# Reordering the first stages of an encoder layer: later surveys, earlier gates, evenly spread side work

## The chip, the cores and the metric

The kernel runs on one core of a Trainium2 chip. The metric is the time of one execution on the device, in microseconds (us). The engines are TensorE (PE in the rows; PEld is its weight load), VectorE (DVE), ScalarE (ACT), GpSimd (POOL) and SyncE (SP), which issues most DMA transfers.

## The reference

One layer of an encoder over 1024 tokens of width 1024, with 256 memory tokens. Only the parts that the first stages of the kernel compute matter here:

```python
h = layer_norm(x, ln_in_w, ln_in_b)
z = h @ w_in + b_in          # q, k, v, o of 4 recurrent heads, 16 gate columns, q, k, v of 8 windowed heads
...
# recurrent heads: both directions, chunks of 128 tokens, log gates summed along the tokens
a = jnp.cumsum(lfc, axis=-1)
m_t = jnp.maximum(inter_log, jnp.max(d_log, axis=-1))
...
ml_out = jax.nn.sigmoid(mo) * (hn * ml_norm_w)
...
# cross-attention of every token into the memory
q = (x @ w_q)...; kv = mem @ w_kv; k, v = jnp.split(kv, 2, axis=-1)
s = jnp.einsum('bthd,bmhd->bhtm', q, k) * (XA_DIM ** -0.5)
o = jnp.einsum('bhtm,bmhd->bthd', p, v).reshape(b, t, d) @ w_o + b_o
```

After it come a gated feed-forward part with a depthwise convolution and a last normalisation. They take most of the kernel's time, and the change does not touch them.

## The kernel before

Almost every float32 product is made from 16-bit or rounded halves: an operand is split into a high half (`whi`, `Be`, `Bo`, ..., by ScalarE, L204 or L571) and a low half (by VectorE, L205, or L572 on VectorE or GpSimd), and a product is three matmuls (L225 high by high, L226 and L227 with one low half) for each slice of 128 rows. A split needs a power-of-two scale for its operand. For a token weight the scale is a short chain: ScalarE and VectorE bound the weight (L309, L311), TensorE spreads the maximum over the partitions (`mx`, L183), and VectorE takes it back (L184) and makes the scale (L175 to L177, L319).

The span before 284 us has two stages.

The **input stage** (L551 to L717) does four things at once. For n from 0 to 15 it makes one slice of the memory's keys or values: weight load L566, split L570 to L572, 24 matmuls into `mem`, eviction L590, maximum L591. It normalises the eight token tiles `x` (norm_a: statistics L238 to L242, a power on GpSimd L243, then L252, L253 on ScalarE, times the weight L256 on VectorE, plus the bias L257 on GpSimd) and transposes and splits them (norm_b: eight transposes L607, split L204 and L205 into `Be` or `Bo`, and the load of tile tt+3, since `x` has three buffers). For n from 8 on it makes the first token product of a tile (tok_item, `tk`, 24 matmuls of 272 columns for gates and values and 24 of 256 columns). And it surveys the cross-attention's weights: a transfer of 1 MB into `cr` (L631) and a maximum over it on VectorE (L633). The first token weight lies in `cr` before that, so a survey comes after its split.

The **chunk stage** (L798 to L840) makes four further chunks c of 256 columns for eight tiles tt: 24 matmuls into `tk`, eviction L814 into `ev`, and for c of 2 and 3 a sigmoid on ScalarE (L819) and a product on GpSimd (L820). Between them it places four kinds of side work, each a generator that is called forward: `kv`, the memory's heads (a weight `wr` of 1 MB L752, its split, matmuls into `mem`, evictions into `stage`, all for one of eight heads); `ts`, the T-sums (ten GpSimd operations L730 to L739 into the single buffer `tsum`, then the halves on ScalarE L742 and VectorE L743; eight groups, two calls each); `gg`, the gates' chain (matmuls L376 to L378, difference `g_sb` L383, transpose L386, a running maximum L394 and L395, rows L406 to L421); and the bounds and splits of the next token weight. `tk` and `mem` share their PSUM banks.

The order in the code is not the order on the engines: a scheduler that runs when the program is built sets each engine's own order from readiness and from the order in which the code emits its work. Each engine then runs its line in order, and an instruction that waits holds all that is queued behind it on that engine; a DMA that waits holds the queue of SP.

Of the kernel before, what the change touches and what calls it, by code (L numbers as in the profile page):

```python
# [56 lines left out]
def encoder(ctx, tc, I, out):  # L57
# [224 lines left out]
    with ExitStack() as ca:  # L282

        yml = None
        with ExitStack() as cm:
# [254 lines left out]
            with ExitStack() as c2:  # L540
# [12 lines left out]
                with ExitStack() as c1:  # L553
# [45 lines left out]
                    def norm_b(tt):  # L599
                        if tt >= NT:  # L600
                            return
                        r = xs.pop(tt)
                        o = slice(tt // 2 * 128, tt // 2 * 128 + 128)
                        for q in range(2):
                            pt = tbank()
                            for k in range(4):
                                T.transpose(pt[:, k, :], r[:, (4 * q + k) * 128:(4 * q + k + 1) * 128], ident)  # L607
                            split16(Bp[tt % 2][:, 0, q, :, o], Bp[tt % 2][:, 1, q, :, o], pt, s0)
                        load_x(tt + 3)
# [62 lines left out]
                    for n in range(8):  # L672
                        if n < 6:
                            split_w(n + 2)
                        if n == 7:
                            split_w(8)
                        kv_item(n)
                        load_w(n + 4)
                        if n == 0:
                            load_x(2)  # L680
                        if n in (2, 3):
                            next(gens[n - 2])
                        if n % 2:
                            norm_a(n // 2)
                            if n > 1:
                                norm_b(n // 2 - 1)
                        if n == 5:
                            next(gens[0])
                        if n == 7:
                            run(gens[0])  # L690
                            next(gens[1])
                    xv = mm.tile([128, 8, 256], F32, name="xvr", tag="xv")
                    for n in range(8, 16):
                        split_w(n + 1)
                        kv_item(n)
                        load_w(n + 4)
                        norm_a(n - 4)
                        norm_b(n - 5)
                        if n == 8:
                            run(gens[1])  # L700
                            nxt = chunk_gen(I["w_tok"][0], 256, cw)
                            next(nxt)
                        if n == 10:
                            pk, sk = scale_of(sums[:, 0:8], 14)
                            as_pairs(xk, "xk", sk, "kp")
                        if n == 15:
                            run(nxt)
                            nxt = chunk_gen(I["w_tok"][1], 256, cw)
                            next(nxt)
                        tok_item(n - 8)  # L710
                        survey(n - 8)
                        if n == 14:
                            next(nxt)
                    pv_, sv_ = scale_of(sums[:, 40:48], 14)
# [83 lines left out]
                with ExitStack() as c1:  # L798
# [5 lines left out]
                    kv, ts, gg, cu0 = kv_gen(), tsum_gen(w1), gate_gen(), cu_prep(0)  # L804
                    next(kv)
                    for c in range(4):
                        w, ic = cw[2 + c]
                        for tt in range(NT):
# [22 lines left out]
                                    next(cu0)  # L831
                            if c == 2 and tt == 4:
                                next(cu0)
                            if c == 1:
                                next(gg, None)
                            with tc.issue_after(d.ins):
                                next(ts, None)
                            if tt in (2, 6):
                                next(kv, None)
                    run(kv)  # L840

# [381 lines left out]
    with ExitStack() as cb_:  # L1223
# [515 lines left out]
        with ExitStack() as cF:  # L1739
# [49 lines left out]
            for tt in range(NT):  # L1789
# [13 lines left out]
                for i in range(2 if last else 1):  # L1803
                    c = slice(i * 512, i * 512 + 512) if last else slice(0, D)
# [88 lines left out]
```

## Time and profile before

| | |
|---|---|
| three runs | 1570.8, 1573.36, 1579.4 us; median 1573.36 |
| profiled execution | 1571.99 us, its span 1570.3 us, mean granted clock 0.976 |
| TensorE busy | 1476.7 us, 94% of the span |
| VectorE, ScalarE, GpSimd busy | 1053.8, 807.4, 574.6 us |
| input stage, chunk stage | 0 to 134.06, 134.06 to 283.74 us |

The rows name an instruction by its line, engine and operation, and by the tiles that it writes and reads (out<-in). A time in brackets is idle time of the engine just before the instruction, with what ended it.

### The profile page before, as it was taken

To read this page: it belongs to the slowest core of one execution; us is meant where nothing else is said; L and a number is where in the kernel's file an instruction comes from. 1 tells how busy PE (TensorE), PEld (TensorE's weight loads), DVE (VectorE), ACT (ScalarE), POOL (GpSimd) and SP (SyncE) were. 2 spreads that over 40 slices of the span, in tenths; PEclk is the share of its full clock that TensorE was granted. 3 is DMA by queue.
4 is the path that set the end of the run, shared out by engine and by line. 5 is a ranking of instruction groups with operands and counts; after the bars stand their busy time and mean duration, and the time that the engine had idled before them with its cause. 6 is when DMAs were issued, how large, how long until landed. Compare 5 with 4: busy or idle time off the path is not lost.

```text
span 1570.3 us, 21752 instructions
## 1 busy us (share of the span) xinstructions
PE 1476.7 (94%) x8134; PEld 881.3 (56%) x8134; DVE 1053.8 (67%) x1961; ACT 807.4 (51%) x1367; POOL 574.6 (37%) x446
## 2 busy tenths in 40 slices
PE   8798889999999899899999889999999999997998
PEld 6697767456766788774455434444444444443443
DVE  7984985445767777675457678788878878925333
ACT  5524544565554467523335668777777756611000
POOL 6423662412232766234112174444434420301342
PEclk9799999999999899999999989999999999998999
DMA  8743545323554743544001332222232434832111
GB/s 297 276 179 112 189 140 190 105 75 101 147 149 130 243 132 102 205 167 180 28 27 54 121 137 108 107 107 108 107 121 107 162 107 144 294 124 69 40 68 54
DMA packets 84896, 208.62 MB, mean 133 GB/s; under 512 B 7091, under 2 KB 36019, under 8 KB 81462
## 3 DMA queue, kind: packets, MB, share of 16 engines
q1 hardware_dynamic: 84496, 206.46, 37.9%
q8 instruction: 64, 1.05, 0.3%
q0 software_dynamic: 144, 0.49, 0.2%
q14 instruction: 42, 0.34, 0.1%
q10 hardware_dynamic: 150, 0.27, 0.0%
HBM read 158.34 MB, written 49.35 MB: 132 GB/s over the span
## 4 chain that ended last, share of the span: by engine, by line
PE 55%; DVE 20%; DMA 9%; ACT 9%; issue 4%; POOL 2%; SPq 1%; DVEq 0%; ACTq 0%; POOLq 0%
PE dn L227 5%; PE dn L226 5%; PE dn L225 5%; DMA sv<-in_w_down_dram 3%; PE S L225 3%; PE S L227 3%; PE S L226 3%; DVE wlo L205 3%; DVE cbuf L1586 2%; DVE cbuf L1587 2%; PE tk L225 2%; PE z L226 2%; PE z L227 2%; PE tk L226 2%; PE tk L227 2%
## 5 line engine op out<-in xcount | busy, mean ns | idle before, releaser
L225 PE MATMUL dn<-whi,yp 128*128 128x512 f16 x336 | 127.6, 383 | 1.4 <-ACT whi L204 1.4
L226 PE MATMUL dn<-wlo,yp 128*128 128x512 f16 x336 | 128.2, 382 | 0.0
L227 PE MATMUL dn<-whi,yp 128*128 128x512 f16 x336 | 128.2, 382 | 0.0
L1504 POOL TENSOR_TENSOR wraw<-ur 128x512 f32<-128x512 f32 x22 | 45.5, 2069 | 201.8 <-issue 187.3
L1586 DVE SCALAR_TENSOR_TENSOR cbuf<-C,wdw,cbuf 128x1024 f32<-128x1024 f32 x44 | 75.7, 1721 | 28.6 <-ACT cbuf L1585 28.5
L225 PEld LDWEIGHTS <-whi 128*128 128x128 f16 x540 | 53.6, 99 | 66.1 <-issue 7.7
L227 PEld LDWEIGHTS <-wlo 128*128 128x128 f16 x540 | 53.4, 99 | 59.8 <-DVE wlo L205 4.2
L226 PEld LDWEIGHTS <-whi 128*128 128x128 f16 x540 | 53.7, 99 | 54.6 <-issue 1.6
L205 DVE SCALAR_TENSOR_TENSOR wlo<-wraw,us,whi 128x1024 f16<-128x1024 f32 (+1 forms) x48 | 67.0, 1413 | 18.8 <-ACT whi L204 18.5
L253 ACT ACTIVATE r<-r,lnrs 128x1024 f32<-128x1024 f32 x19 | 23.6, 1243 | 101.7 <-DVE lnrs L252 101.7
L1587 DVE SCALAR_TENSOR_TENSOR cbuf<-C,wdw,cbuf 128x1024 f32<-128x1024 f32 x44 | 70.5, 1602 | 1.2
L204 ACT ACTIVATE whi<-wraw,us 128x1024 f16<-128x1024 f32 (+1 forms) x48 | 51.4, 1103 | 27.2 <-DVE us L177 22.3
L225 PEld LDWEIGHTS <-yp 128*128 128x128 f16 x352 | 34.6, 98 | 52.1 <-issue 11.5
L1585 ACT ACTIVATE cbuf<-C,bdw,wdw 128x1024 f32<-128x1024 f32 x44 | 54.5, 1238 | 10.5 <-DVE C L1622 9.7
L243 POOL TENSOR_TENSOR lnrs<-lnrs,mhalf 128x1 f32<-128x1 f32 x32 | 18.8, 589 | 110.7 <-DVE lnrs L242 93.1
L227 PEld LDWEIGHTS <-yp 128*128 128x128 f16 x352 | 34.6, 98 | 42.4 <-issue 1.4
L226 PEld LDWEIGHTS <-yp 128*128 128x128 f16 x352 | 34.7, 99 | 42.2 <-issue 1.4
L225 PE MATMUL tk<-whi,Bo 128*128 128x256 f16 (+1 forms) x192 | 53.6, 279 | 3.1 <-DVE stage L205 3.1
L226 PE MATMUL tk<-wlo,Be 128*128 128x256 f16 (+1 forms) x192 | 53.6, 279 | 2.1 <-DVE wlo L205 2.1
L225 PE MATMUL tk<-whi,Be 128*128 128x256 f16 (+1 forms) x192 | 53.9, 282 | 0.3 <-ACT whi L204 0.3
L227 PE MATMUL tk<-whi,Be 128*128 128x256 f16 (+1 forms) x192 | 53.6, 279 | 0.0
L226 PE MATMUL tk<-wlo,Bo 128*128 128x256 f16 (+1 forms) x192 | 53.2, 277 | 0.0
(496 smaller groups left out, 4855.4 us busy)
## 6 DMA issues: line engine op xcount, KB each, us to landing
ur<-in_w_up_dram SPq DMA_DIRECT2D x22, 1024.0 KB
sv<-in_w_down_dram SPq DMA_DIRECT2D x22, 512.0 KB
y<-cbuf SPq DMA_DIRECT2D x22, 512.0 KB
ur<-y SPq DMA_DIRECT2D x11, 1024.0 KB
wraw<-in_w_down_dram SPq DMA_DIRECT2D x22, 512.0 KB
r<-h SPq DMA_DIRECT2D x19, 512.0 KB
h<-r SPq DMA_DIRECT2D x16, 512.0 KB
wraw<-in_w_tok_dram SPq DMA_DIRECT2D x10, 512.0 KB
```

What stands on the lines that cost most here:

```text
L204: A.activation(hi, src, AF.Copy, scale=s)
L205: return V.scalar_tensor_tensor(lo, src, s, hi, op0=OP.mult, op1=OP.subtract)
L225: T.matmul(ps, lh, rh, start=first, stop=False, skip_group_check=skip)
L226: T.matmul(ps, lh, rl, start=False, stop=False, skip_group_check=skip)
L227: return T.matmul(ps, ll, rh, start=False, stop=last, skip_group_check=skip)
L243: G.tensor_tensor(rs[:, 0:1], rs[:, 0:1], mhalf[:, 0:1], OP.pow)
L253: A.activation(r, r, AF.Identity, scale=rs[:, 0:1], bias=rs[:, 1:2])
L1504: G.tensor_tensor(S1, A21, A22, OP.add)
L1585: A.activation(c, C[:, 1:SEQ + 1], AF.Identity, scale=wdw[:, 1, j:j + 1], bias=bdw[:, j:j + 1])
L1586: V.scalar_tensor_tensor(c, C[:, 0:SEQ], wdw[:, 0, j:j + 1], c, op0=OP.mult, op1=OP.add)
L1587: V.scalar_tensor_tensor(c, C[:, 2:SEQ + 2], wdw[:, 2, j:j + 1], c, op0=OP.mult, op1=OP.add)
```

## The change

No instruction is added or removed. In the input stage only tiles 0 to 2 are normalised, and only tile 0 is transposed, before n = 8; from then on a tile is normalised two steps before it is transposed. The surveys are placed at n from 10 to 15, the last four in pairs, instead of one at each n from 8 on. In the chunk stage the gates' chain is called at every second tile of the chunks 0 and 1 instead of at every tile of chunk 1; the T-sums at every odd tile of all four chunks instead of at every tile of the first two; the memory's heads at every second to fourth product instead of at two tiles of each chunk.

```diff
-                        if n % 2:
+                        if n in (1, 3, 5):
                             norm_a(n // 2)
-                            if n > 1:
-                                norm_b(n // 2 - 1)
                         if n == 5:
+                            norm_b(0)
                             next(gens[0])
...
-                        norm_a(n - 4)
-                        norm_b(n - 5)
+                        norm_a(n - 5)
+                        norm_b(n - 7)
...
-                        survey(n - 8)
+                        for i in {10: (0,), 11: (1,), 12: (2,), 13: (3,), 14: (4, 5), 15: (6, 7)}.get(n, ()):
+                            survey(i)
...
-                            if c == 1:
+                            if c < 2 and tt % 2 == 0:
                                 next(gg, None)
-                            with tc.issue_after(d.ins):
-                                next(ts, None)
-                            if tt in (2, 6):
+                            if tt % 2:
+                                with tc.issue_after(d.ins):
+                                    next(ts, None)
+                            if 8 * c + tt in (6, 10, 13, 16, 19, 22, 25, 28):
                                 next(kv, None)
```

On VectorE, where the scale of the first token weight is made (L184 to L319, with `us` the scale and `cr` the weight), this stood before:

```order
L184 TENSOR_REDUCE us<-mx 128x1
L242 TENSOR_SCALAR lnrs<-lnmv 128x1
L591 TENSOR_REDUCE sums<-xvr 128x1
L175 TENSOR_SCALAR us<-us 128x1
L238 BN_STATS lnst<-x 128x6 x2
L176 TENSOR_SCALAR us<-us 128x1
L240 BN_AGGR lnmv<-lnst 128x2
L177 TENSOR_SCALAR us<-us 128x1
L319 TENSOR_SCALAR us<-us,sc 128x1
L242 TENSOR_SCALAR lnrs<-lnmv 128x1
L252 TENSOR_SCALAR lnrs<-lnmv,lnrs 128x1 x2
L205 SCALAR_TENSOR_TENSOR wlo<-cr,us,whi 128x1088 x2
```

and this stands there now:

```order
L591 TENSOR_REDUCE sums<-xk 128x1
L572 TENSOR_TENSOR wlo<-wr_136,whi 128x1024
L591 TENSOR_REDUCE sums<-xk 128x1
L184 TENSOR_REDUCE us<-mx 128x1
L175 TENSOR_SCALAR us<-us 128x1
L176 TENSOR_SCALAR us<-us 128x1
L177 TENSOR_SCALAR us<-us 128x1
L319 TENSOR_SCALAR us<-us,sc 128x1
L591 TENSOR_REDUCE sums<-xk 128x1
L238 BN_STATS lnst<-x 128x6 x2
L311 TENSOR_TENSOR l_527<-l_527 128x1
L205 SCALAR_TENSOR_TENSOR wlo<-cr,us,whi 128x1088
```

The five steps of the scale now follow each other, between the maxima of the memory's keys instead of those of its values (`xk` comes before `xvr`). On TensorE the `mx` product of this scale stands behind 170 matmuls of the memory's slices, where before there were 218 and 24 transposes. The second token weight's scale still has other work between its steps: L184, L242, a survey's L633, L175.

On VectorE, at the gates' difference `g_sb` in the chunk stage, this stood before, in chunk 1:

```order
L205 SCALAR_TENSOR_TENSOR wlo<-wr,sc,whi 128x1024 x2
L814 SCALAR_TENSOR_TENSOR ev<-tk,us,btok_1473 128x256
L743 TENSOR_TENSOR TX1l<-tsum,TX1l 128x256 x2
L743 TENSOR_TENSOR TX1h<-tsum,TX1h 128x256
L814 SCALAR_TENSOR_TENSOR ev<-tk,us,btok_1473 128x256
L743 TENSOR_TENSOR TX1h<-tsum,TX1h 128x256
L380 COPY a_sb<-s 128x64
L381 COPY aend<-s 1x64
L383 TENSOR_TENSOR g_sb<-gates,a_sb 128x32 x2
```

and this stands there now, in chunk 0:

```order
L814 SCALAR_TENSOR_TENSOR ev<-tk,us,btok_1473 128x256
L380 COPY a_sb<-s 128x64
L381 COPY aend<-s 1x64
L383 TENSOR_TENSOR g_sb<-gates,a_sb 128x32 x2
L205 SCALAR_TENSOR_TENSOR wlo<-wr,sc,whi 128x1024
L814 SCALAR_TENSOR_TENSOR ev<-tk,us,btok_1473 128x256
L743 TENSOR_TENSOR TX1l<-tsum,TX1l 128x256
L743 TENSOR_TENSOR TX1h<-tsum,TX1h 128x256
L205 SCALAR_TENSOR_TENSOR wlo<-wr,sc,whi 128x1024
L814 SCALAR_TENSOR_TENSOR ev<-tk,us,btok_1473 128x256
L390 COPY cx_1689<-s 64x128
L311 TENSOR_TENSOR l_1555<-l_1555 128x1
```

The gates' difference now stands in front of the first memory head's split, and L311 of a coming token weight behind it. On TensorE the first memory product comes after seven token products of the stage instead of three.

On GpSimd the end of the chunk stage read before, behind the last group of T-sums:

```order
L736 TENSOR_TENSOR tsum<-Bo,tsum 128x256
L737 TENSOR_TENSOR tsum<-tsum,Bo 128x256
L738 TENSOR_TENSOR tsum<-Be,tsum 128x256
L739 TENSOR_TENSOR tsum<-tsum,Be 128x256
L820 TENSOR_TENSOR ev<-ev,mlw 128x256 x16
L471 TENSOR_TENSOR ev_3209<-wraw 128x512
```

and reads now:

```order
L734 TENSOR_TENSOR tsum<-tsum,Bo 128x256
L820 TENSOR_TENSOR ev<-ev,mlw 128x256
L732 TENSOR_TENSOR tsum<-tsum,Be 128x256
L735 TENSOR_TENSOR tsum<-tsum,Bo 128x256
L736 TENSOR_TENSOR tsum<-Bo,tsum 128x256
L737 TENSOR_TENSOR tsum<-tsum,Bo 128x256
L738 TENSOR_TENSOR tsum<-Be,tsum 128x256
L739 TENSOR_TENSOR tsum<-tsum,Be 128x256
L820 TENSOR_TENSOR ev<-ev,mlw 128x256 x3
L471 TENSOR_TENSOR ev_3209<-wraw 128x512
```

All sixteen L820 stood behind the last group; thirteen of them now stand within or between the last four groups.

## Rows read from the trace of the kernel before

**Rows 1.** TensorE's waits from 0 to 284 us, without those that a later group shows in the timeline alone or that the change doesn't meet: the waiting matmul, what it waited for, us in total, times, the longest.

```profile
PE mem L225 <- ACT whi L204: 5.5, 1, 5.5
PE tp L607 <- POOL x L257: 4.3, 2, 3.7
PE s L386 <- DVE g_sb L383: 4.2, 1, 4.2
...
PE tk L225 <- DVE stage L205: 3.1, 1, 3.1
...
PE mx L183 <- DVE l L311: 1.6, 1, 1.6
PE mem L225 <- ACT whi L571: 1.5, 1, 1.5
...
PE mem L225 <- DVE ev L814: 0.6, 1, 0.6
```

**Rows 2.** Busy time of each engine by stretch, with the granted clock of TensorE behind them, then the DMA share and GB/s. The columns: stretch, its length, then PE, PEld, DVE, ACT and POOL, each busy us and (instructions).

```profile
31.33:57.54 26.21, 20.42 (x149) 19.80 (x150) 21.74 (x41) 16.90 (x26) 14.11 (x8) 0.83 0.64 229
57.54:76.02 18.48, 14.33 (x90) 11.44 (x90) 18.39 (x28) 7.00 (x11) 7.05 (x4) 0.78 0.91 335
76.02:134.06 58.04, 58.04 (x496) 52.43 (x496) 40.58 (x63) 16.97 (x24) 16.99 (x16) 0.97 0.37 137
...
148.22:186.65 38.43, 34.25 (x300) 29.91 (x301) 30.63 (x49) 21.99 (x37) 23.87 (x27) 0.94 0.63 201
186.65:235.25 48.60, 43.10 (x341) 34.30 (x342) 40.84 (x91) 24.83 (x44) 31.88 (x38) 0.95 0.40 127
```

**Rows 3.** The timeline of TensorE at the first token product: start, duration, instruction, idle time before it.

```profile
53.05 1.97 PE L607 MATMUL tp<-ident,x 128*128 128x128 f32 x8 [3.72 <-POOL x L257]
...
57.54 0.38 PE L226 MATMUL tk<-wlo,Be 128*128 128x272 f16 x1 [2.07 <-DVE wlo L205]
```

**Rows 4.** The timeline of VectorE at the same place, with the first token weight's scale (`us`) and the split that it serves.

```profile
50.33 0.28 DVE L184 TENSOR_REDUCE us<-mx 128x1 f32<-128x128 f32 x1
...
50.98 1.27 DVE L238 BATCH_NORM_STATS2 lnst<-x 128x6 f32<-128x512 f32 x2
...
52.43 0.20 DVE L319 TENSOR_SCALAR us<-us,sc 128x1 f32<-128x1 f32 x1
...
54.18 4.57 DVE L205 SCALAR_TENSOR_TENSOR wlo<-cr,us,whi 128x1088 f16<-128x1088 f32 x2
```

**Rows 5.** Three stretches of 5 us, with the columns of rows 2.

```profile
55.00:60.00 5.00, 2.93 (x15) 1.74 (x13) 5.00 (x4) 3.25 (x4) 1.38 (x2) 0.50 0.40 119
...
185.00:190.00 5.00, 3.35 (x16) 2.42 (x17) 4.66 (x12) 1.89 (x2) 4.76 (x8) 0.51 0.72 274
205.00:210.00 5.00, 2.87 (x27) 2.58 (x28) 5.00 (x10) 2.12 (x4) 3.51 (x4) 1.00 0.79 285
```

**Rows 6.** The timeline of TensorE at its second long wait in the input stage.

```profile
72.33 1.88 PE L607 MATMUL tp<-ident,x 128*128 128x128 f32 x8 [3.13 <-DVE us L176]
```

**Rows 7.** The timeline of VectorE before it, with the second token weight's scale.

```profile
67.42 0.28 DVE L184 TENSOR_REDUCE us<-mx 128x1 f32<-128x128 f32 x1
...
68.21 2.27 DVE L633 TENSOR_REDUCE sums<-cr 128x1 f32<-128x2048 f32 x1
...
74.02 0.20 DVE L319 TENSOR_SCALAR us<-us,sc 128x1 f32<-128x1 f32 x1
```

**Rows 8.** VectorE's costliest line of the input stage, by line: count, busy us, mean ns of one, idle time before.

```profile
L633 DVE TENSOR_REDUCE sums<-cr 128x1 f32<-128x2048 f32 x8 | 18.1, 2267 | 0.0
```

**Rows 9.** The timeline of TensorE at its three long waits of the chunk stage.

```profile
148.22 0.39 PE L225 MATMUL mem<-xkp,whi 128*128 128x256 f16 x1 [5.46 <-ACT whi L204]
...
186.65 0.39 PE L386 MATMUL s<-ident,g_sb 128*64 128x128 f32 x1 [4.18 <-DVE g_sb L383]
...
207.13 0.28 PE L225 MATMUL tk<-whi,Bo 128*128 128x256 f16 x1 [3.14 <-DVE stage L205]
```

**Rows 10.** The timeline of VectorE at the split of the first memory head's weight.

```profile
148.19 2.98 DVE L205 SCALAR_TENSOR_TENSOR wlo<-wr,sc,whi 128x1024 f16<-128x1024 f32 x2 [3.64 <-ACT whi L204]
```

**Rows 11.** The timeline of TensorE at the end of the input stage: the first of the last token product's 24 matmuls, and the matmul that follows the last.

```profile
131.44 0.27 PE L225 MATMUL tk<-whi,Bo 128*128 128x256 f16 x1
...
134.06 0.61 PE L183 MATMUL mx<-ident,sc 128*128 128x128 f32 x4
```

**Rows 12.** The timeline of VectorE before the gates' transpose.

```profile
179.71 3.17 DVE L205 SCALAR_TENSOR_TENSOR wlo<-wr,sc,whi 128x1024 f16<-128x1024 f32 x2 [1.15 <-ACT whi L204]
...
185.28 1.23 DVE L383 TENSOR_TENSOR g_sb<-gates,a_sb 128x32 f32<-128x32 f32 x2
```

**Rows 13.** The timeline of VectorE before the third long wait of the chunk stage.

```profile
201.06 1.27 DVE L205 SCALAR_TENSOR_TENSOR wlo<-wraw,us,whi 128x1024 f16<-128x1024 f32 x1
202.26 2.46 DVE L205 SCALAR_TENSOR_TENSOR wlo<-wr,sc,whi 128x1024 f16<-128x1024 f32 x2
```

**Rows 14.** The timeline of GpSimd at the end of the chunk stage.

```profile
285.02 0.72 POOL L820 TENSOR_TENSOR ev<-ev,mlw 128x256 f32<-128x256 f32 x1 [7.08 <-ACT ev L819]
```

**Rows 15.** Single operations in the timeline of GpSimd: L736 of two T-sum groups, and an L820.

```profile
119.26 0.69 POOL L736 TENSOR_TENSOR tsum<-Bo,tsum 128x256 f32<-128x256 f16 x1
...
201.08 4.18 POOL L736 TENSOR_TENSOR tsum<-Bo,tsum 128x256 f32<-128x256 f16 x1
...
254.17 1.25 POOL L820 TENSOR_TENSOR ev<-ev,mlw 128x256 f32<-128x256 f32 x1 [4.62 <-ACT ev L819]
```

## The prediction, made before the changed kernel had run

> **What bounds the kernel now.** I began with the waits of TensorE over the first 284 us, because the change touches nothing later, then cut that time by stage, and then read VectorE, ScalarE and GpSimd around each long wait. By the waits [rows 1] TensorE stands still there some 33 us in all, and each long wait is ended by another engine's result, not by a transfer: by a split weight, a normalised tile, a scale, the gates. The stages [rows 2] show where: 149.7 us belong to the token products and the memory's heads (134.06 to 283.74), and the 45 us from 31.33 to 76.02 belong to the input stage, in which VectorE is busy 40.1 of 44.7 us while TensorE is busy 34.8. From 76.02 to 134.06 TensorE is busy throughout. What the change can win lies in two clusters: TensorE waiting for a saturated VectorE before 76 us, and TensorE waiting for things that come in bursts from 142 to 216 us.
>
> **Input stage.** Nothing is added or removed; instructions change places. At the first token product TensorE waits 3.72 us for a normalised tile and, after eight transposes, 2.07 us for the low half of the weight [rows 3]. Behind the second wait stands a chain on VectorE [rows 4]: its first step, the maximum over mx, begins at 50.33, the scale is finished at 52.63, and the split that follows is done at 58.75. Between those steps stand a normalisation's statistics (1.27 us), its aggregate and its L242, which belong to later tiles; the first product's own transposes wait for the tile's L256 and L257 behind them. In the order of the changed kernel the chain L184, L175, L176, L177, L319 is undivided and tiles 1 and 2 are normalised after it. Transposes of tiles 1 to 3 no longer precede the first product.
>
> So the first token product can start as soon as its weight is split. I carried the rows forward in the new order: the mx product falls after 170 instead of 218 products of the memory's inputs and 24 transposes; the first token product comes at about 48.1 us instead of 57.54, 9.4 us earlier, an estimate. Of these, 2.0 us are eight transposes at 1.97 us per eight [rows 3], which are only postponed. That leaves 7.4. The same from the other side: the two waits are 5.79 us, and while TensorE recovers its granted clock is 0.50 from 55 to 60 us [rows 5], where 2.93 us of busy work would take half at the upper level, 1.5 us more: 7.3.
>
> What is late next: the second cluster. It waits 3.13 us in front of the next transposes [rows 6], because the second chain on VectorE is spread from 67.42 to 74.22 [rows 7], with a survey of 2.27 us in the middle and two splits of transposed tiles and an L256 behind it. The new order still has a survey inside this chain (L184, L242, L633, L175), since the order is made from readiness and not from the place in the code. So I leave the second cluster where it is. The surveys cost VectorE 18.1 us, eight at 2267 ns [rows 8]; moving them helps only as far as they really leave the saturated time. New waits also come: a tile's transposes stand in front of token products with one product's lead, so each may wait for a normalised tile, as one does now for 0.6 us (4.3 less the longest, 3.7), or for a weight's high half, 1.5 us [rows 1]. I charge one of each, 2.1 us. Sum of the stage: -7.4 + 2.1 = -5.3. Bounds: if the second cluster's 3.13 us go too and nothing new comes, -10.5; if new waits take as much as the old ones and two weight waits more, +2.
>
> **Token products and memory's heads.** Three long waits lie here [rows 9]: 5.46 us before the first memory product, 4.18 us before the gates' transpose, 3.14 us before a token product; 0.6 us more is mem behind ev [rows 1]. The first: VectorE's half of the weight's split begins at 148.19, after 3.64 us of idle time for ScalarE's half [rows 10], while the memory product comes after three token products in TensorE's line. In the new order seven token products of 24 matmuls come first instead of three. The product before the stage's end takes 2.62 us (131.44 to 134.06, [rows 11]), so four more cover 10.5 us, more than the 5.46. The second wait: the gates' difference g_sb at 185.28 stands on VectorE behind a weight's split of 3.17 us, two evictions and the sums' low halves [rows 12]. In the new order it comes right behind its own inputs, in front of the first split of a memory head. The third, before 207.13, stands behind VectorE's splits of 1.27 us for a token weight and 2 x 1.2 for a memory head in one burst [rows 13], with the gates' rows between them; with heads at every third product the burst is divided. All four: 5.46 + 4.18 + 3.14 + 0.6 = 13.4 us.
>
> Clock: after the 4.18 us wait the granted clock is 0.51 from 185 to 190 us, yet 1.00 after the 3.14 us wait [rows 5]. Over the two stretches from 148.22 to 235.25 it is 0.94 and 0.95 [rows 2], which is 0.06 x 38.4 + 0.05 x 48.6 = 4.7 us if TensorE had work all that time. I count 3 of them as gone.
>
> New waits: VectorE now takes the first memory weight's split in front of evictions and of l_1555. When that split waits for its transfer, as it does now for 3.64 us, what is queued behind it is late: the evictions free the banks that token products write, and L311 feeds the mx product, which sits in TensorE's line. I price that at 1.8, the old mx wait being 1.6 [rows 1], plus 1.1 for the scan's result behind evictions and 0.7 for the second token weight of each chunk; between 2 and 3 us stay for the other four gaps of this size that I can't place, and 1 for the clock after them. Together 6.6 (from 2 to 13, since eight memory heads each bring one place to wait). Sum: -13.4 - 3 + 6.6 = -9.8. Bounds -15 and -3.
>
> Sums and S-preparation: GpSimd's sums now lie beside the products of chunks 2 and 3, so its last group ends late; in the order, three products' L820 and then L471 come behind it. The last L820 waits for the last product now too (285.02), and L471 stands behind it in both orders [rows 14]; a T-sum is needed by TensorE only much later. So I add nothing; if the last group is late, its delay goes through L471 to L474 to a split that TensorE waits for, and I take the 3.5 us by which the slowest L736 exceeds one alone as the bound [rows 15]. Everything after 284 us: 0, with a bound of 1 each way.
>
> Total on the profiled execution: 1571.99 - 5.3 - 9.8 = 1556.9. It lies 1.4 us under the median of the three runs, so the forecast for the median is 1558 us.
>
> **A rule against it.** The row: a T-sum operation takes 0.69 us when alone, and 4.18 us, L736, while VectorE runs three splits from 201.06 to 204.72 [rows 13, 15]. In the Trainium skill, SBUF — State Buffer, section "SBUF: two separate sides", VectorE and GpSimd share a port pair as an exclusive lock: an operation of VectorE with two SBUF inputs, or one of GpSimd that reads SBUF, takes it for its whole length and the other waits. The trace agrees: 4.18 is about 0.69 and the 3.66 us of the three splits. By that rule each of the four sum groups that now lie beside heads would grow by a head's split, 2.98 us [rows 10], 12 us of GpSimd's time that my sum has at nothing; it is the ground of rival B.
>
> **Rivals.** A: the input stage gains nothing. For it: VectorE is saturated (18.39 of the 18.48 us behind 57.54, [rows 2]), surveys are still pulled early, and the x loads stand behind more transposes in SP's queue. Against: the first chain is undivided. Then only the second stage pays: 1573.4 - 8 to -10, about 1565. C: the second stage's waits only change places (the ring of bank, eviction and split remains, and its work is the same), while the first pays: 1573.4 - 5, about 1568.
>
> B, slower: T-sums hold the in-order lines of chunks 2 and 3. A group has one buffer. VectorE's L743 waits for ScalarE's copy, which waits for the group; behind L743 stands an eviction, and the token products need its bank. Now GpSimd's line also has L820 inside the groups, each waiting for a sigmoid that ScalarE runs after that eviction. If a group lasts longer than the four products between its calls, it is paid by TensorE: a group of ten at 0.67 is 6.7 us, one worst operation adds 3.5 and two L820 under contention 2.5 (1.25 each, [rows 15]), so 6.0 more in each of four groups, 24 us, and at half clock after each wait some 1.7 us more: 31. From 1558 that gives 1589. It decides from the point at which three groups are late. Against it: four products are 10.5 us and 1.25 heads about 6 us more, so 16 us, and the longest group now is 11.5 us; it needs waits that chain up.
>
> **How the numbers follow.** Forecast 0.62, with own range 1548 to 1566; A 0.16; C 0.12; B 0.10. The median of three runs, 1573.36, moves 0.5% at 7.9 us, about what a measurement of this kernel tells from no change: 1565.5 and 1581.2. Faster: nearly all of the forecast (0.59) and half of A, 0.67. Same: the rest of these and C, 0.23. Slower: B, 0.10. The range reaches to C and to B's lower half: 1547 to 1577; beyond it lie about 0.08 of B and 0.07 of better outcomes.
>
> **What would show it.** Right: the waits before the first token product (transposes behind L257, token product behind the low half) are together under 2 us and it starts near 48; the 3.13 us wait is still there; the first memory product and the gates' transpose wait under 1 us; the stage from the first chunk's product to its end lasts about 140 us instead of 149.7; the stage after it is as before. Wrong: if VectorE's idle time before 100 us doesn't change and TensorE's waits there sum to 17 us again (A); if TensorE waits in chunks 2 and 3 behind L814 or L743 (B); if the second stage is still 148 us or longer (C).

## The result and the profile after

The changed kernel takes 1559.53 us, the median of six runs (1554.76 to 1562.55), against 1574.11 for the kernel before in six; the ratio is 0.9903, its 95% interval 0.9881 to 0.9926. So the change wins 14.6 us, and the forecast of 1558 lies 1.5 us under the measured median. The profiled execution of the changed kernel took 1562.55 us, span 1560.8. One of the ten executions of a later kernel, normalisation and heads, took 2869.94 us at a granted clock of 0.837 and is in no number here.

To compare stages, one mark is used throughout: the first matmul of the recurrent state (`stb`), which stands behind the same 3797 matmuls and weight loads on TensorE in every kernel here. It starts at 335.4 us in the kernel before and at 323.4 in the changed one, as the summary of this tile shows, of before and then of the changed kernel (durations in ns, first and last start in us):

```profile
L868 PE MATMUL stb<-V,kw x56: 272/275/276, 335.4 to 373.4; 128*128 128x129 f32 x56
...
L869 PE MATMUL stb<-V,kw x56: 272/275/276, 323.4 to 361.4; 128*128 128x129 f32 x56
```

Twelve microseconds are won there. From the mark to the end the profiled execution of before needs 1236.6 us and that of the changed kernel 1239.2; over the fourteen profiles of this study this rest lies between 1233 and 1242 us. In the two kernels that were profiled twice the mark repeats within 1.4 and 0.5 us, the whole execution within 1.6 and 5.5.

TensorE's waits up to 284 us, with the columns of [rows 1]:

```profile
PE s L403 <- DVE gm L400: 4.1, 1, 4.1
PE tp L607 <- DVE Be L205: 3.6, 2, 2.9
PE mem L227 <- DVE wlo L572: 3.1, 1, 3.1
PE tp L607 <- POOL x L257: 2.9, 2, 2.2
...
PE mem L225 <- DVE stage L205: 2.2, 1, 2.2
PE mem L225 <- ACT whi L571: 1.8, 1, 1.8
PE mx L183 <- DVE l L311: 1.5, 1, 1.5
PE tk L225 <- ACT whi L204: 1.4, 1, 1.4
```

The waits behind the first memory weight (5.5), the gates' difference (4.2), the first token weight's low half (2.1) and the third wait of the chunk stage (3.1) are gone. So is the old wait of an mx product behind `l`, 1.6 us at 215.44 [rows 1]; the one listed now lies at 150.35, at another place of the stage. New are 4.1 us behind `gm`, the result of the gates' running maximum, and 2.2 behind a `stage`. The stages in the changed kernel, with the columns of [rows 2]:

```profile
31.89:48.46 16.57, 16.57 (x129) 16.56 (x130) 11.37 (x22) 9.64 (x17) 8.32 (x4) 0.90 0.73 255
48.46:65.53 17.07, 12.04 (x96) 10.53 (x94) 15.25 (x30) 9.60 (x14) 6.45 (x5) 0.91 0.88 328
65.53:129.76 64.23, 61.98 (x512) 55.19 (x512) 48.79 (x80) 21.74 (x30) 27.82 (x20) 0.94 0.44 162
129.76:158.93 29.17, 23.61 (x214) 20.71 (x213) 20.82 (x65) 12.69 (x20) 7.70 (x10) 0.98 0.45 157
158.93:220.00 61.07, 58.84 (x489) 49.93 (x490) 42.46 (x86) 34.57 (x58) 26.68 (x33) 0.92 0.66 200
220.00:274.00 54.00, 54.00 (x396) 38.66 (x395) 34.48 (x63) 27.94 (x54) 31.16 (x44) 1.00 0.45 165
```

TensorE now works without a gap from 31.89 to 48.46, where it begins the first token product; before, it did so at 54.81 and was stopped until 57.54 [rows 3]. The input stage ends at 129.76 instead of 134.06. The chunk stage ends with the first matmul into `cu`, at 272.14 instead of 283.74, so it lasts 142.38 us instead of 149.68. The two chunk stages as a whole, before and after:

```profile
134.06:283.74 149.68, 134.54 (x1088) 107.87 (x1087) 103.65 (x211) 74.83 (x130) 71.68 (x85) 0.97 0.51 169
...
129.76:272.14 142.38, 134.59 (x1088) 108.42 (x1087) 96.52 (x207) 74.71 (x130) 64.13 (x84) 0.96 0.53 176
```

TensorE is busy for the same time in both, at about the same clock: what the stage wins is waiting time. The timeline of TensorE at the waits that are left:

```profile
48.46 0.28 PE L225 MATMUL tk<-whi,Be 128*128 128x272 f16 x1
...
59.07 0.63 PE L607 MATMUL tp<-ident,x 128*128 128x128 f32 x4 [0.71 <-DVE Be L205]
...
62.63 1.09 PE L607 MATMUL tp<-ident,x 128*128 128x128 f32 x4 [2.94 <-DVE Be L205]
...
65.53 0.37 PE L225 MATMUL tk<-whi,Be 128*128 128x256 f16 x1 [1.39 <-ACT whi L204]
...
95.56 0.66 PE L607 MATMUL tp<-ident,x 128*128 128x128 f32 x4 [2.23 <-POOL x L257]
...
158.93 0.37 PE L403 MATMUL s<-ident,gm 64*1 64x64 f32 x2 [4.05 <-DVE gm L400]
...
178.22 0.27 PE L225 MATMUL mem<-xkp,whi 128*128 128x256 f16 x1 [2.23 <-DVE stage L205]
```

And VectorE around the first three waits, with the second token weight's scale and the splits of a transposed tile (`Be`):

```profile
55.34 0.28 DVE L184 TENSOR_REDUCE us<-mx 128x1 f32<-128x128 f32 x1
...
55.60 2.28 DVE L633 TENSOR_REDUCE sums<-cr 128x1 f32<-128x2048 f32 x1
...
58.18 0.74 DVE L205 SCALAR_TENSOR_TENSOR Be<-tp,sc,Be 128x512 f16<-128x512 f32 x1
...
58.84 2.27 DVE L633 TENSOR_REDUCE sums<-cr 128x1 f32<-128x2048 f32 x1
...
61.75 0.74 DVE L205 SCALAR_TENSOR_TENSOR Be<-tp,sc,Be 128x512 f16<-128x512 f32 x1
...
63.12 0.20 DVE L319 TENSOR_SCALAR us<-us,sc 128x1 f32<-128x1 f32 x1
```

Two surveys stand between the first and the last step of this scale, which take 8.0 us together (55.34 to 63.32), against 6.8 before with one survey [rows 7]. The same two surveys stand in front of two splits of a transposed tile, and it is these splits, done at 58.92 and 62.49, that end the waits of 0.71 and 2.94 us. On the scale hangs the third wait, 1.39 us for the weight's high half.

### The profile page after: what moved, and what is told of

It is laid out like the page before. It is cut to its first block, busy times and chain, and to the rows that moved or that the text cites. A ratio compares the mean times of both kernels' runs of the same rounds, so it can differ in the third digit from the quotient of the medians.

```text
span 1560.8 us, 21755 instructions
## 1 busy us (share of the span) xinstructions
PE 1476.6 (95%) x8134; PEld 879.3 (56%) x8134; DVE 1045.2 (67%) x1961; ACT 807.2 (52%) x1367; POOL 573.3 (37%) x446
## 4 chain that ended last, share of the span: by engine, by line
PE 52%; DVE 22%; DMA 9%; ACT 9%; issue 4%; POOL 4%; SPq 1%; DVEq 0%; ACTq 0%; POOLq 0%
PE dn L226 5%; PE dn L227 5%; PE dn L225 5%; PE S L225 3%; PE S L227 3%; PE S L226 3%; DMA sv<-in_w_down_dram 3%; DVE wlo L205 3%; DVE cbuf L1587 3%; DVE cbuf L1588 2%; PE z L226 2%; PE z L225 2%; PE z L227 2%; PE cl L225 2%; PE cl L226 2%
## 5 line engine op out<-in xcount | busy, mean ns | idle before, releaser
L205 DVE SCALAR_TENSOR_TENSOR wlo<-wraw,us,whi 128x1024 f16<-128x1024 f32 (+1 forms) x48 | 67.6, 1425 | 17.7 <-ACT whi L204 17.4
L204 ACT ACTIVATE whi<-wraw,us 128x1024 f16<-128x1024 f32 (+1 forms) x48 | 51.3, 1103 | 17.5 <-DVE us L177 11.3
L1586 ACT ACTIVATE cbuf<-C,bdw,wdw 128x1024 f32<-128x1024 f32 x44 | 54.5, 1238 | 10.6 <-DVE C L1623 9.8
L1182 ACT ACTIVATE P<-P,mn 128x256 f32<-128x256 f32 (+1 forms) x64 | 35.6, 557 | 33.3 <-DVE mn L1180 33.1
```

Of the source, the lines that this page charges most:

```text
L204: A.activation(hi, src, AF.Copy, scale=s)
L205: return V.scalar_tensor_tensor(lo, src, s, hi, op0=OP.mult, op1=OP.subtract)
L1182: A.activation(P[:, :nk], P[:, :nk], AF.Exp, scale=-1.0, bias=mn[:, 0:1], accum_out=mn[:, 1:2])
L1586: A.activation(c, C[:, 1:SEQ + 1], AF.Identity, scale=wdw[:, 1, j:j + 1], bias=bdw[:, j:j + 1])
```

## Experiments

All orders compared here are those in which the built program has each engine's instructions. A first finding needs no run: the kernel before with the surveys' edit alone has, on each of the five engines, the same order as the kernel before, and the changed kernel without that edit the same order as with it. The edit in the code moves no instruction.

The table collects what the runs gave; the diffs and expectations follow. "Rest" is the profiled time less the mark; each ratio is to the runs of before that were taken beside the kernel.

| kernel | median us (runs) | ratio to before, 95% | `stb` at | rest |
|---|---|---|---|---|
| before | 1573.02 to 1574.15 (13 to 17 in each of three sets) | | 335.4 | 1236.6 |
| changed | 1559.53 (6) | 0.9903, 0.9881 to 0.9926 | 323.4 | 1239.2 |
| changed, again | 1560.75 (6) | 0.9918, 0.9897 to 0.9940 | 322.0 | 1238.9 |
| normalisation alone | 1567.07 (9) | 0.9963, 0.9944 to 0.9983 | 328.5 | 1238.2 |
| chunk stage alone | 1566.20 (7) | 0.9966, 0.9948 to 0.9984 | 327.2 | 1238.5 |
| gates undone | 1556.81 (4) | 0.9902, 0.9876 to 0.9927 | 323.4 | 1233.2 |
| sums undone | 1561.00 (4) | 0.9923, 0.9904 to 0.9942 | 325.7 | 1233.9 |
| heads undone | 1570.45 (10) | 0.9986, 0.9972 to 0.9999 | 335.2 | 1238.3 |
| normalisation and heads | 1570.04 (9) | 0.9969, 0.9954 to 0.9984 | 332.3 | 1237.9 |
| surveys held | 1548.83 (4) | 0.9855, 0.9823 to 0.9888 | 311.5 | 1234.6 |
| surveys behind the chain | 1548.99 (4) | 0.9836, 0.9808 to 0.9864 | 311.4 | 1238.5 |
| gap in the gates | 1558.64 (4) | 0.9906, 0.9880 to 0.9932 | 317.6 | 1241.3 |
| gap, again | 1556.41 (6) | 0.9889, 0.9868 to 0.9910 | 317.1 | 1236.3 |
| surveys held and gap | 1541.73 (4) | 0.9799, 0.9785 to 0.9814 | 305.4 | 1236.3 |

**The two halves apart.** The first has only the normalisation's lines of the change, the second only those of the chunk stage:

```diff
-                        if n % 2:
+                        if n in (1, 3, 5):
...
-                        norm_a(n - 4)
-                        norm_b(n - 5)
+                        norm_a(n - 5)
+                        norm_b(n - 7)
```

> The kernel before with the later normalisation alone; each engine's order of the input stage is then the same as with the moved surveys beside it. Theory (the two halves are independent, and the input half is the normalisation's): the first token product starts near 48.5 us, the input stage ends near 129.8 (before 134.06), the chunk stage after it is as before, 155 us to the first L498, total 4 to 5 us under before. Rival (the moved surveys carry the input half): the input stage ends at 133 to 134 us and the total is that of before.

> The kernel before with the gates, the T-sums and the memory's heads as changed, the input stage as before. Theory: the input stage ends at 134 us as before, the stretch from there to the first L498 lasts some 148 us instead of 155, the waits of 5.5 and 4.2 us (memory product, gates' transpose) are gone, a wait for gm of 3 to 5 us is there; total 7 to 8 us under before. Rival (the chunk stage gains only because the input stage hands over its tiles and x loads in another way): under 3 us gained.

Both theories hold, though the normalisation alone wins more than the 4 to 5 us expected. It starts the first token product at 48.7 us, the mark comes 6.9 us earlier, the median is 6.8 lower. The chunk stage alone leaves the product at 54.9 and moves the mark by 8.2, the median by 7.6. The two sum to 15.1 us at the mark; the whole change gives 12.0 in its first profile and 13.4 in its second, and 14.6 and 13.4 in the medians. The halves add up within what the runs tell. Up to the chunk stage the kernel with the normalisation alone has the same order on each engine as the changed one, so three profiles show one input stage: it ends at 129.76 and 128.74 in the two of the changed kernel and at 128.34 here.

**The three parts of the chunk stage.** Each is undone alone; the last kernel has only the heads beside the normalisation.

```diff
-                            if c < 2 and tt % 2 == 0:
+                            if c == 1:
                                 next(gg, None)
```

> The changed kernel with the gates' chain at every tile of chunk 1 again. Theory (the gates' part trades a wait of 4.2 us behind g_sb for one of 4.1 behind gm, so it is worth little): a wait behind g_sb of 1 to 4 us returns, the one behind gm is under 1; stb between 322 and 326, total within 2 us of the changed kernel. Rival (the early chain is what frees VectorE for the heads): stb at 328 or later, total 4 us or more above the changed kernel.

```diff
-                            if tt % 2:
-                                with tc.issue_after(d.ins):
-                                    next(ts, None)
+                            with tc.issue_after(d.ins):
+                                next(ts, None)
```

> The changed kernel with T-sums at every tile of chunks 0 and 1 again. Theory (the sums' spread costs and gives little, since GpSimd and ScalarE have room in both): stb between 322 and 327, total within 3 us of the changed kernel. Rival (the sums' low halves on VectorE beside the running maximum and the splits are what the chunk stage's waits come from): stb at 328 or later, a wait behind L743 or a split of 2 us or more in chunk 1.

```diff
-                            if 8 * c + tt in (6, 10, 13, 16, 19, 22, 25, 28):
+                            if tt in (2, 6):
                                 next(kv, None)
```

> The changed kernel with the memory's heads at two tiles of each chunk again. Theory (the heads' spread carries the chunk stage's gain): the wait before the first memory product, 5.5 us before, returns with 3 to 6 us, and one of 2 to 4 us behind a burst of splits; stb at 328 to 332, total 4 to 8 us above the changed kernel. Rival (once the gates are early the first head is hidden anyway): stb under 326, total within 2 us.

> The later normalisation and the spread heads, with the gates' chain and the T-sums as in the kernel before. Theory (the heads carry the chunk stage's gain, and the moved gates and sums only keep out of their way): stb at 321 to 327 (normalisation alone 328.5, all 323.4), total 1557 to 1564. Rival (the three parts only work together): stb at 330 or later, total 1566 or more.

The first two agree with their theories: without the gates' part the mark stays at 323.4 and the median is 2.7 us lower, inside the spread of either; a wait of 3.7 us behind `g_sb` is back as expected, and one of 4.9 behind `ev` that was not, in place of the two behind `gm` and `stage`. Without the sums' part the mark is 2.3 us later, little more than the 1.4 by which it repeats. Without the heads' it is 11.8 us later, at 335.2, where 328 to 332 was expected. Of this 7.3 us are the whole gain of the chunk stage, which lasts 149.72 us there, and 5.0 lie behind it: from the first `cu` to the mark that kernel needs 56.3 us, the changed one 51.3.

The fourth run refutes the theory that the heads carry the gain alone: beside the normalisation only, they put the mark at 332.3, 3.8 us behind the normalisation alone, in one profile each; the medians, 1570.04 and 1567.07, lie the same way, but the intervals of their ratios overlap. The heads gain only beside the sums or the gates. Beside the normalisation (328.5), the heads alone cost 3.8 us, the gates with the sums cost 6.7, and the heads win 5.1 with the sums, 2.8 with the gates and 5.1 with both. So the gates' part adds nothing that these runs can tell once the other two are in place. Where the heads alone lose is seen from 160 to 220 us. The kernel with normalisation and heads:

```profile
160.00:220.00 60.00, 47.17 (x363) 38.27 (x362) 47.50 (x101) 27.41 (x50) 43.65 (x50) 0.86 0.47 153
```

and the changed kernel:

```profile
160.00:220.00 60.00, 57.77 (x485) 49.27 (x483) 41.93 (x82) 33.64 (x58) 26.68 (x33) 0.93 0.67 201
```

With the heads alone VectorE is busy 47.5 us there and GpSimd 43.7, since the T-sums and the gates' chain still have their place in the first two chunks; TensorE is busy 10.6 us less and its clock is lower. Its waits there, in the same kernel's timeline, are all behind VectorE:

```profile
184.77 0.37 PE L403 MATMUL s<-ident,gm 64*1 64x64 f32 x2 [5.54 <-DVE gm L400]
...
195.50 0.27 PE L225 MATMUL tk<-whi,Bo 128*128 128x256 f16 x1 [2.38 <-DVE ev L814]
...
206.22 0.43 PE L419 MATMUL s<-rows,ones 1*128 1x64 f32 x2 [2.34 <-DVE rows L416]
```

With the heads undone the splits come in bursts again, 5.23 us before the first memory product and 5.41 before a token product:

```profile
143.59 0.40 PE L225 MATMUL mem<-xkp,whi 128*128 128x256 f16 x1 [5.23 <-ACT whi L204]
...
197.61 0.39 PE L225 MATMUL tk<-whi,Bo 128*128 128x256 f16 x1 [5.41 <-DVE stage L205]
```

That the heads need the room that the sums or the gates leave is read from these waits. No run isolates which operation of VectorE is displaced.

**Surveys that really move.** The maximum of each survey is held on VectorE behind an eviction: in the first kernel behind that of its own token product, in the second only behind the first tile's, directly after the scale chain.

```diff
-                        tok_item(n - 8)
+                        last = tok_item(n - 8)
                         for i in {10: (0,), 11: (1,), 12: (2,), 13: (3,), 14: (4, 5), 15: (6, 7)}.get(n, ()):
-                            survey(i)
+                            with tc.issue_after(last.ins):
+                                survey(i)
```

> The changed kernel with each survey's maximum held on VectorE behind the eviction of the token product after which the code places it, so that the surveys really move. Theory (two surveys inside the second token weight's scale chain are what TensorE waits for from 57 to 66 us): the 2.9 us wait of the transposes behind Be and the 0.7 us before it go, the 1.4 us behind the weight's high half shrinks, the input stage ends 3 to 6 us earlier (124 to 127 us), total 3 to 6 us under the changed kernel, if the scales of the surveys aren't late for the first memory head. Rival (VectorE is saturated there whatever comes first): another wait of 3 to 5 us takes the place, total within 1 us of the changed kernel.

> The changed kernel with all surveys held on VectorE only behind the first tile's second eviction: they leave the second token weight's scale chain, but stand right behind it, still in VectorE's full stretch before 100 us. Theory (the place inside the chain is what costs, not VectorE's load): the 2.9 us wait behind Be and the lower clock from 60 to 100 us go as with the surveys held to their own tiles; stb at 311 to 315 (changed kernel 323.4, held 311.5), total 1548 to 1552. Rival (VectorE's load before 100 us costs): other waits of 3 to 5 us in front of transposes or token products come between 66 and 100 us; stb at 317 to 323, total 1554 to 1560.

The two kernels put the mark at 311.5 and 311.4, some 12 us before the changed kernel (10.6 before its second profile), and their medians are 10.7 and 10.5 us under its first median, 11.9 and 11.8 under its second. Of the first kernel 3 to 6 us were expected, and an end of the input stage at 124 to 127 us; it ends at 117.66. The chunk stage is as long as in the changed kernel, 142.7 us, so the gain is the input stage's. The chain is now undivided, as VectorE's timeline shows in the kernel with held surveys:

```profile
54.66 0.28 DVE L184 TENSOR_REDUCE us<-mx 128x1 f32<-128x128 f32 x1
...
55.42 0.20 DVE L319 TENSOR_SCALAR us<-us,sc 128x1 f32<-128x1 f32 x1
```

It takes 1.0 us instead of 8.0. The three waits of 0.71, 2.94 and 1.39 us are gone, 5.0 us, and with them the lower clock: from 60 to 80 us the changed kernel shows

```profile
60.00:80.00 20.00, 15.97 (x117) 13.61 (x118) 19.75 (x26) 5.87 (x7) 4.66 (x2) 0.83 1.01 380
```

and the one with held surveys

```profile
60.00:80.00 20.00, 20.00 (x179) 18.38 (x178) 18.17 (x29) 8.40 (x11) 9.61 (x5) 1.00 0.67 238
```

TensorE does 179 matmuls instead of 117, at a clock of 1.00 instead of 0.83. From 80 to 100 us the changed kernel is at 0.91, and waits 2.23 us at 95.56 for the sixth tile. That tile's statistics begin on VectorE at 71.39 and its L256 at 88.59, with three surveys in between, and its L257 stands on GpSimd behind an L572 of 5.78 us that ends at 93.20. With the surveys held that wait is 0.7 or less. The second kernel decides between the theories: its surveys stand in the same saturated stretch (VectorE is busy 39.7 of the 40 us from 60 to 100) and TensorE is busy 39.5 of the same 40, against 33.7 in the changed kernel, which comes first here:

```profile
60.00:100.00 40.00, 33.74 (x257) 29.20 (x258) 39.75 (x58) 14.92 (x19) 17.02 (x7) 0.87 0.79 290
...
60.00:100.00 40.00, 39.50 (x347) 36.33 (x344) 39.73 (x59) 16.18 (x22) 14.54 (x8) 1.00 0.78 278
```

So it was the place of the surveys, not VectorE's load. What that place holds up is not isolated. Both kernels take the surveys out of the scale's chain and from in front of the tile's splits at once, and the scheduler answers on other engines too: of the eight transposes and the mx product that the changed kernel has right in front of the first product with the second token weight (59.07 to 65.53), four transposes are left there, and SP issues the next token weight's two transfers at 58.30 and 62.73 in the kernel with held surveys, ahead of the surveys' transfers, instead of at 70.36 and 73.88.

**A gap before the result of the gates.** The calls of the gates' chain at tiles 0, 2, 4 of both chunks, instead of 0, 2, 4, 6 and 0, 2:

```diff
-                            if c < 2 and tt % 2 == 0:
+                            if 8 * c + tt in (0, 2, 4, 8, 10, 12):
                                 next(gg, None)
```

> The changed kernel with the gates' chain called at tiles 0, 2, 4 of chunk 0 and 0, 2, 4 of chunk 1, so that the product that takes gm (L403) stands two token products later. Theory (TensorE meets L403 before VectorE's running maximum is done): the 4.05 us wait behind gm falls to under 0.5 and the half clock after it (0.52 from 160 to 165 us) goes, 3 to 6 us under the changed kernel. Rival (VectorE's line is what is late, and what stands behind the running maximum waits instead): a wait of 2 to 4 us appears at an mx product or a weight's low half in its place, total within 1 us of the changed kernel.

> The kernel with the gap before L403 once more, with more rounds and beside the changed kernel on the same chip. Its profile had stb 5.8 us earlier than the changed kernel's, its median only 0.9 us lower. Theory (the gain at stb is real and the rest of the profiled execution varies by some us from run to run): 4 to 7 us under the changed kernel. Rival (what is won before stb is given back behind it): within 2 us of the changed kernel, with the time from stb to the end 3 us or more longer.

> The changed kernel once more, as the partner of the kernel with the gap on the same chip and to see how far a profile repeats: stb within 1 us of 323.4 and the waits of the first 284 us within 0.5 us each; the time from there to the end between 1234 and 1241; median 1556 to 1562.

The wait behind `gm` is gone in both profiles, and the mark comes 5.8 and 4.9 us earlier than in the changed kernel's two. Of new waits, those behind a low half `wlo` sum to 3.2 us, but the one behind `stage` is gone too. The first median was only 0.9 us lower, but no run of the changed kernel stood beside it, and its profiled execution has the longest rest of all, 1241.3 us. Run beside the changed kernel the median is 4.3 us lower, and the rest, 1236.3, is the shorter of the two. So the gain is real, about 4 us in the time and 5 to 6 at the mark, and the rival that it is given back later falls. The changed kernel itself did not repeat as closely as expected: its mark came at 322.0, 1.4 us off where 1 was allowed. From 95 to 100 us its clock is 0.66 in the first profile, behind the wait at 95.56, and 1.00 in the second, where that wait is 1.9 us; that alone is 0.34 x 5 = 1.7 us, the price that rival B put on the clock after a wait.

> The changed kernel with both edits: surveys held behind their token products, and the gates' chain with a gap before L403. In the profiles the first state matmul (stb) starts at 323.4 in the changed kernel, 311.5 with the held surveys, 317.6 with the gap. Theory (the two waits are independent): the 1.6 us wait behind gm goes too, stb at 306 to 310, total 1543 to 1548. Rival (with VectorE taking the surveys from 75 to 125 us, its line in the chunk stage is so full that the gap only moves the wait): stb at 310 to 313, total as with the held surveys, 1547 to 1551.

Both edits together give 1541.73 us, 31 us under the kernel before (0.9799, 0.9785 to 0.9814) and 18 to 19 under the changed kernel, which did not run beside it; the mark is at 305.4, 18.0 earlier. The two gains add up: 11.9 and 5.8 sum to 17.7.

## Why the prediction was right

The time and its two terms hold in the main: -5.3 for the input stage against 4.3 and 5.3 us won at its end in the two profiles of the changed kernel and 5.7 with the normalisation alone, and -9.8 for the chunk stage against 7.3 at its end, 7.7 at the mark and 8.2 at the mark with the chunk stage alone. That the total came within 1.5 us is in part luck: the terms sum to -15.1, the profiles show 12.0 and 13.4 at the mark, and the time behind the mark, whose change was put at 0 with a bound of 1, runs from 1233 to 1242 us over the profiles here.

- *The first token product.* Forecast near 48.1, without the two waits: 48.46, without them. That the later normalisation does this was shown by the kernel that has it alone (48.7); no run separates the undivided chain from the postponed transposes. (The forecast counted from 57.54, where the product of before goes on; it had begun at 54.81.)
- *The surveys.* That they would still be pulled early, and the second cluster stay, was right: 2.94 us stand for the 3.13 of before, and two surveys are in the chain. The reason was not quite right: the transposes do not need the scale. They wait for the split of the tile before, in the changed kernel and before too, where that split is done at 72.18, behind the survey that begins at 68.21 [rows 7]. The line is from the kernel before:

```profile
71.44 0.74 DVE L205 SCALAR_TENSOR_TENSOR Be<-tp,sc,Be 128x512 f16<-128x512 f32 x1
```

Its worth was underrated. The prediction gave 3.13 us as what it could yield, without the clock; holding the surveys back yields 11.9.
- *The four waits of the chunk stage.* Forecast 13.4 us removed: all four are gone. The first memory product and the gates' transpose wait for nothing, and the stage lasts 142.4 us where about 140 was named as the sign.
- *The new waits.* The mx product behind l was priced at 1.8 and waits 1.51, but in place of the old one of 1.6, which the sum had left standing. The term that failed is the wait behind the scan's result, priced at 1.1: TensorE met L403 4.05 us early. After the gates' transpose, at 144.21, TensorE has 53 matmuls of token products and 24 of the first memory product in front of L403, and with the wait of 1.51 us it is through at 154.88. VectorE takes up the transpose's result only at 149.44, behind the two splits of that head's weight, the sums' low halves and two evictions, and needs from 150.22 to 158.78, 8.6 us, for the running maximum and its end, with evictions and a scale between:

```profile
150.22 0.27 DVE L394 TENSOR_TENSOR cx<-cx 32x128 f32<-32x128 f32 x1
...
153.26 0.65 DVE L395 TENSOR_TENSOR cx<-cx 32x128 f32<-32x128 f32 x1
...
157.70 0.28 DVE L395 TENSOR_TENSOR cx<-cx 32x128 f32<-32x128 f32 x1
158.02 0.48 DVE L814 SCALAR_TENSOR_TENSOR ev<-tk,us,btok 128x256 f32<-128x256 f32 x1
...
158.64 0.14 DVE L400 COPY gm<-cx 32x1 f32<-32x1 f32 x1
```

Seven of the fourteen operations of the running maximum take 0.64 to 0.72 us instead of 0.27 or 0.28. All seven lie beside a group of T-sums on GpSimd (148.08 to 156.02); with no such operation beside them, as with the gates undone, all fourteen take 0.28. That is 2.8 us of the 4.05, an estimate from these rows; no run moves the group alone. So the contention that the prediction charged to GpSimd under rival B shows on VectorE here.

- *The clock.* 3 of 4.7 us were counted as gone. They are not: the stretch from 158.93 to 220.00 is at 0.92, 0.08 x 61.1 = 4.9 us, as after the wait behind `gm` the clock is at 0.52 again, from 160 to 165 us, and the whole stage is at 0.96 where it was at 0.97. The 2 to 3 us kept for waits without a place came as one, 2.23 us behind a `stage`. Redone with what was measured, the term is: waits of before 14.9 us, with the old mx wait; waits now 4.05 + 2.23 + 1.51 = 7.8; clock nothing; together -7.1, against 7.3 measured. The forecast's -9.8 differs by the clock (2.0 us, 3 given back less 1 charged), by new waits of 7.8 where it had 5.6, and the other way by the 1.6 of the old wait.
- *The sums.* Priced at nothing, and rival B at 1589. TensorE is busy without a gap from 220 to 274 us, where three of the four groups with L820 lie; the first of the four runs from 209.85 to 219.75, 9.9 us, the longest of all eight groups and under the 16 that B needs. The last line is the split on VectorE beside it:

```profile
209.85 0.67 POOL L730 TENSOR_TENSOR tsum<-Bo,Be 128x256 f32<-128x256 f16 x1 [2.70 <-DVE TX1h L743]
210.47 1.65 POOL L733 TENSOR_TENSOR tsum<-Bo 128x256 f32<-128x256 f16 x1
...
219.08 0.67 POOL L739 TENSOR_TENSOR tsum<-tsum,Be 128x256 f32<-128x256 f32 x1
...
210.08 3.13 DVE L205 SCALAR_TENSOR_TENSOR wlo<-wr,sc,whi 128x1024 f16<-128x1024 f32 x2
```

Two operations beside that split take 1.65 and 1.64 instead of 0.67 us, so the group grew by 2.0 us and not by the split's whole length. The lock that the Trainium skill states (SBUF — State Buffer, "SBUF: two separate sides") is compatible with that, but the splits no longer come three in a row, and no operation of 4.18 us [rows 15] is left.

Rival A fell with the input stage's 4.3 us, rival C with the chunk stage's 7.3. One thing was not foreseen: the prediction took each wait of the chunk stage as removed by the part that names it, and the runs show that the heads give their gain only beside the sums or the gates.

## What to carry to other kernels

Where a scheduler sets the engines' order, moving lines of code need not move work: compare the built orders first, and where an instruction must come later, tie it to one that does. A long operation of VectorE in front of small ones that TensorE needs, the steps of a scale or the split of a transposed tile, costs their wait and the clock behind that wait; the same operation a few microseconds later cost nothing that shows here, on an engine that stayed just as full. Side work is to be tried as a set: one generator moved into a stretch where others still stand won nothing here, and by the profile lost 3.8 us, while with another one it won 2.8 to 5.1.

## What was not expected

Holding the surveys back removed 5.0 us of waits between 59 and 66 us and gave 11.9 us at the mark. Most of the difference is the granted clock: 0.83 from 60 to 80 us and 0.91 from 80 to 100 became 1.00, which is at most 0.17 x 20 + 0.09 x 20 = 5.2 us; 1.5 more are the later wait for the sixth tile, 2.23 less 0.7. And two executions of one program differ more behind the mark than before it: the kernel with the gap had the mark at 317.6 and 317.1, but 1241.3 and 1236.3 us behind it.
